# Attention over windows of 64 rows: VectorE and ScalarE as loops of three units with token semaphores, spare loads copied by GpSimd, stores issued later in the unit

## The chip, the cores and the metric

The kernel runs on one core of a Trainium2 chip. Sixteen DMA engines move data between HBM (the large memory) and the buffers on the chip; a transfer is *issued* by an instruction, waits its turn in a queue (18.9 to 29.2 us from issue to landing for v, q, k and the store, medians on the page of the kernel before), and has *landed* when all its data is there. The metric is the device time of one execution in microseconds (us), the median of several. The span printed on a profile page is some 1.8 us shorter than the device time of the same execution.

Executions of one and the same kernel scatter by about 2 us each way, and now and then by more. The times below are always given with the kernel before timed on the same chip in the same rounds.

## The reference

```python
# q, k, v: float32 [4, 4096, 1536]; windows of W = 64 rows
q_w, k_w, v_w = (x.reshape(B, S // 64, 64, D) for x in (q, k, v))
logits = einsum('bnwd,bnud->bnwu', q_w, k_w) * D ** -0.5
attn   = softmax(logits, axis=-1)
out    = einsum('bnwu,bnud->bnwd', attn, v_w).reshape(B, S, D)
```

Three inputs of 100.66 MB are read and one output of the same size is written. There is little arithmetic for each byte.

## The kernel before

The 16384 rows are cut into N = 32 units of 512 rows. For each unit:

1. GpSimd (POOL) issues loads of q, k and v, 3.15 MB each in HBM, on one queue that casts to fp16 on the way. `q16`, `k16` and `v16` have one buffer each, so a load can be issued only after TensorE (PE) has finished with the unit before.
2. PE transposes q and k; VectorE (DVE) and ScalarE (ACT) copy the results in turns to `xq` and `xk`; PE forms the logits; ACT takes exp.
3. The last stage has four rows, n = 0 to 3. In each, PE multiplies with v into three 128x512 outputs, with one more matmul for the sum of the exps. DVE takes the reciprocal of the sum, and DVE and ACT scale the outputs into one of three `outs` buffers.
4. POOL issues the store of the unit, 3.15 MB.

The first loads have special places, because nothing has come free yet: q and k of unit 1 go to `outs[2]`, v of unit 1 to `outs[1]`, v of unit 2 to `vs`. DVE copies them to `q16`, `k16` and `v16`. The parts that matter (cuts are marked `# ...`):

```python
def vector_unit(u):                        # unrolled, 32 times
    # ... six copies of transposes, waits on counts: p_t >= 6*u + ...
    src = {1: staged(1, 0), 2: vs, N - 1: vs}.get(u)
    if src is not None:                    # spare load of v
        # ... waits
        ve.tensor_copy(out=v16[:, :, :], in_=src[:, :, :]).then_inc(g_v, 1)
    if u == 0:                             # spare load of q
        ve.wait_ge(d_q1, 16)
        ve.wait_ge(p_t[1], 3)
        ve.tensor_copy(out=q16[:, :, :], in_=staged(2, 0)).then_inc(g_q, 1)
    for n in range(H * R):                 # the four rows of the last stage
        ve.wait_ge(p_s, 4 * u + n + 1)     # the sum is there
        ve.reciprocal(...).then_inc(n_r, 1)    # both DVE and ACT wait for n_r
        # ... scale DVE's share of the three outputs, each after its own p_o
    if u == 0:
        # ... the same for the spare load of k

# PE, last stage: the sum matmul follows the first output of each row
for j in range(NJ):
    # ... matmul of output j
    if j == 0:
        # ... sum matmul, tells p_s

# POOL
for u in range(1, N):
    gp.wait_ge(p_t[1], 6 * u + 3);  load("q", u + 1, q16, d_q)
    gp.wait_ge(p_t[1], 6 * u + 6);  load("k", u + 1, k16, d_k)
    store(u - 1)                           # waits for the scaling of unit u-1
    gp.wait_ge(p_o[0], 6 * u + 6); gp.wait_ge(p_o[1], 6 * u + 6)
    load("v", u + 1, v16, d_v)             # 2 < u + 1 < N - 1
```

The whole kernel:

The softmax here doesn't subtract the row's maximum and nothing guards it: scores larger than these inputs give would overflow.

Of the kernel before, what the change touches and what calls it, by code (L numbers as in the profile page):

```python
# [17 lines left out]
def kernel(  # L18
# [13 lines left out]
    PE = mybir.EngineType.PE  # L32
# [31 lines left out]
    zeros = sb("zeros", [P, 1], FP32)  # L64
# [12 lines left out]
    g_q, g_k, g_v, g_w = (sem(n) for n in ("g_q", "g_k", "g_v", "g_w"))  # L77
# [6 lines left out]
    n_r = sem("n_r")  # L84
# [45 lines left out]
    def tensor_unit():  # L130
        def transpose(g):
            src = q16 if g < DC else k16
            c = g % DC
            for i in range(SLOTS):
                r, j = i // H, i % H
                pairs = src[:, R * j + r, :].bitcast(FP32)
                if g == DC and i == 0:
                    nc.tensor.sem_inc(g_k, -1)._wait_ge(g_k, 1)
                ins = nc.tensor.transpose(  # L139
                    tps[g % 2][:, r, j, :], pairs[:, c * P : (c + 1) * P], ident[:, :]  # L140
                )
                if i == 0 and g >= 2:
                    ins._wait_ge(f_c[(g - 2) % 4], 1).then_inc(f_c[(g - 2) % 4], -1)
                if g == 0 and i == 0:
                    ins._wait_ge(g_q, 1)
                if g == 0 and i == 1:
                    ins.then_inc(g_q, -1)
                if i == SLOTS - 1:
                    ins.then_inc(p_t[g % 2], 1)

        def product(c):
            for h in range(H):
                for w in range(2):
                    for r in range(R):
                        ins = nc.tensor.matmul(  # L155
                            lts[h][:, r, :, :],
                            lhsT=halves(xk, c)[:, r, h, :, w],
                            rhs=halves(xq, c)[:, :, h, :, w],
                            start=(c == 0 and w == 0 and r == 0),
                            stop=(c == DC - 1 and w == 1),  # L160
                            skip_group_check=True,
                        )
                        if h == w == r == 0 and c >= DC - 2:
                            s = f_c[(DC + c) % 4]
                            ins._wait_ge(s, 1).then_inc(s, -1)
                        if c == DC - 1 and w == r == 1:
                            ins.then_inc(p_l, 1)

        for g in range(2 * DC):
            transpose(g)  # L170
            if g >= DC + 2:
                product(g - DC - 2)
        product(DC - 2)
        product(DC - 1)
        for n in range(H * R):
            h, t = n // R, n % R
            if n == 0:
                nc.tensor.sem_inc(g_v, -1)._wait_ge(g_v, 1)  # L178
            for r in range(R):
                w = ets[h][:, r, t, :]  # L180
                ld = nc.tensor.ldweights(w)  # L181
                if r == 0 and t == 0:
                    ld._wait_ge(f_x[h], 1)
                for j in range(NJ):
                    ins = reuse(
                        ops[j][:, :], w, v16[:, R * h + r, 512 * j : 512 * (j + 1)], r == 0, r == R - 1
                    )
                    if r == 0:
                        if n == 0 and j == 0:
                            ins._wait_ge(g_w, 1).then_inc(g_w, -1)  # L190
                        elif n > 0:
                            ins._wait_ge(f_o[j][n % 2], 1).then_inc(f_o[j][n % 2], -1)
                    if r == R - 1:
                        ins.then_inc(p_o[on_act(n, j)], 1)
                    if j == 0:
                        ins = reuse(sp[:, n : n + 1], w, ones[:, 0:1], r == 0, r == R - 1)
                        if r == 0 and t == 0:
                            ins.then_inc(f_x[h], -1)
                        if r == R - 1:
                            ins.then_inc(p_s, 1)  # L200

    def copy_out(eng, copy, u, g):
        xt = xq if g < DC else xk
        eng.wait_ge(p_t[g % 2], 6 * u + g // 2 + 1)
# [7 lines left out]
    def freed(eng, u):  # L212
        if u >= NO:
            eng.wait_ge(d_o[u % NO], 16 * (u // NO))

    def told(ins, n, j, a):
        if n == H * R - 1:
# [4 lines left out]
    def vector_unit(u):  # L222
        ve = nc.vector
        for g in range(0, 2 * DC, 2):
            copy_out(ve, ve.tensor_copy, u, g)
        src = {1: staged(1, 0), 2: vs, N - 1: vs}.get(u)
        if src is not None:
            ve.wait_ge(*((d_v1, 16) if u == 1 else (d_vs, 16 if u == 2 else 32)))
            ve.wait_ge(p_o[0], 6 * u)
            ve.wait_ge(p_o[1], 6 * u)  # L230
            ve.tensor_copy(out=v16[:, :, :], in_=src[:, :, :]).then_inc(g_v, 1)
        if u == 0:
            ve.wait_ge(d_q1, 16)
            ve.wait_ge(p_t[1], 3)
            ve.tensor_copy(out=q16[:, :, :], in_=staged(2, 0)).then_inc(g_q, 1)
        i = 0
        for n in range(H * R):
            ve.wait_ge(p_s, 4 * u + n + 1)
            ve.reciprocal(out=rs[:, n : n + 1], in_=sp[:, n : n + 1]).then_inc(n_r, 1)  # L239
            for j in range(NJ):  # L240
                if not on_act(n, j):
                    if i == 0:
                        freed(ve, u)
                    ve.wait_ge(n_r, 4 * u + n + 1)
                    ve.wait_ge(p_o[0], 6 * u + i + 1)
                    i += 1
                    told(
                        ve.tensor_scalar_mul(scaled(u, n, j), ops[j][:, :], scalar1=rs[:, n : n + 1]),  # L248
                        n, j, 0,
                    )  # L250
        if u == 0:
            ve.wait_ge(d_k1, 16)
            ve.wait_ge(p_t[1], 6)
            ve.tensor_copy(out=k16[:, :, :], in_=staged(2, 1)).then_inc(g_k, 1)

    def scalar_unit(u):
        sc = nc.scalar
        for g in range(1, 2 * DC, 2):
            copy_out(sc, sc.copy, u, g)
        for h in range(H):  # L260
            sc.wait_ge(p_l, 2 * u + h + 1)
            for a in range(0, P, W // R):
                s = slice(a, a + W // R)
                ins = sc.activation(  # L264
                    ets[h][s, :, :, s], lts[h][s, :, :, s], EXP, bias=zeros[s, :], scale=scale
                )
            ins.then_inc(f_x[h], 1)
        i = 0
        for n in range(H * R):
            for j in range(NJ):  # L270
                if on_act(n, j):
                    if i == 0:
                        freed(sc, u)
                    sc.wait_ge(n_r, 4 * u + n + 1)
                    sc.wait_ge(p_o[1], 6 * u + i + 1)  # L275
                    i += 1
                    told(
                        sc.activation(  # L278
                            scaled(u, n, j), ops[j][:, :], COPY, bias=0.0, scale=rs[:, n : n + 1]
                        ),  # L280
                        n, j, 1,
                    )

    def store(u):
        gp = nc.gpsimd
        gp.wait_ge(n_e[0], 2 * u + 2)
        gp.wait_ge(n_e[1], u + 1)
        gp.dma_start(  # L288
            out=rows(of, u * UR, SLOTS, R), in_=slots(outs[u % NO], 0, SLOTS, R)
        ).then_inc(d_o[u % NO], 16)  # L290

    with tc.tile_critical(no_gpsimd_drain=True):
# [26 lines left out]
        nc.scalar.activation(rs[:, 0:1], zeros[:, :], EXP, bias=zeros[:, :], scale=1.0)  # L319
# [8 lines left out]
        for u in range(N):  # L328
            vector_unit(u)
            scalar_unit(u)  # L330

        sy = nc.sync
        sy.sem_inc(g_w, 1)
# [3 lines left out]
        sy.wait_ge(d_k, 16)  # L337
        sy.sem_inc(g_k, 1)
        sy.wait_ge(d_v, 16)
        sy.sem_inc(g_v, 1)  # L340
        for u in range(1, N + 1):
            if 1 < u < N:
                sy.wait_ge(d_q, 16 * (u - 1))
                sy.sem_inc(g_q, 1)
                sy.wait_ge(d_k, 16 * u)
                sy.sem_inc(g_k, 1)
            if u < N:
                sy.wait_ge(n_e[0], 2 * u)
                sy.wait_ge(n_e[1], u)
                sy.sem_inc(g_w, 1)  # L350
            if 2 < u < N - 1:
                sy.wait_ge(d_v, 16 * (u - 1))
                sy.sem_inc(g_v, 1)

        gp = nc.gpsimd
        for u in range(1, N):
            if u + 1 < N:
                gp.wait_ge(p_t[1], 6 * u + 3)
                load("q", u + 1, q16, d_q)
                gp.wait_ge(p_t[1], 6 * u + 6)  # L360
                load("k", u + 1, k16, d_k)
            if u + 1 == N - 1:
                load("v", u + 1, vs, d_vs)
            store(u - 1)
            if 2 < u + 1 < N - 1:
                gp.wait_ge(p_o[0], 6 * u + 6)
                gp.wait_ge(p_o[1], 6 * u + 6)
                load("v", u + 1, v16, d_v)


        u, base, o = N - 1, (N - 1) * UR, outs[(N - 1) % NO]
        gp.wait_ge(p_o[1], 6 * u + 5)
        gp.wait_ge(p_o[0], 6 * u + 4)
        gp.dma_start(out=rows(of, base, R, R), in_=slots(o, 0, R, R)).then_inc(d_l[0], 16)
        gp.wait_ge(p_o[1], 6 * u + 6)
        gp.wait_ge(p_o[0], 6 * u + 6)
# [3 lines left out]
        for j, (a, c) in enumerate(((0, 2 * N - 1), (1, N), (0, 2 * N))):  # L380
# [43 lines left out]
```

## Time and profile before

| | before |
|---|---|
| device time, median of 3 | 948.83 us (948.52 to 949.06) |
| span of the profiled execution | 948.6 us |
| HBM traffic | 301.99 MB read, 100.66 MB written |
| mean rate over the span | 424 GB/s |
| PE / ACT / DVE / POOL busy | 67 / 36 / 32 / 9% |

The first lines of the page, the row of DMA digits (each the mean busy share of the DMA engines in one fortieth of the span, in tenths), and the line of HBM traffic, before:

```profile
span 948.6 us, 10199 instructions
...
PE 631.6 (67%) x4096; PEld 349.9 (37%) x3328; DVE 301.4 (32%) x524; ACT 341.2 (36%) x644; POOL 81.8 (9%) x133
...
DMA  9999999999999999999999999999999999999997
...
HBM read 301.99 MB, written 100.66 MB: 424 GB/s over the span
```

The row of nines is the main reading: the sixteen DMA engines are busy from the first slice to the last, and the busiest other engine, PE, is at 67%. From the packet records I read a steady rate of about 431 GB/s in the middle of the run, with reads counted at their size in HBM. A load writes only half of what it reads (fp16 for fp32), and it still takes as long as a store: 7.24 to 7.32 us of the queue for a load, 7.34 us for a store (medians, kernel before). So the time goes by the size in HBM here, and no run here shows which part of the path is the limit; that the transfers alone set the time is shown below (e4). The gap between 424 over the span and 431 is start, drain and a few short deficits.

Two groups of instructions, before: line, engine, operation, count, then busy time, mean ns, the idle time just before them and what ended most of it.

```profile
L114 PE MATMUL o<-v,et 128*128 128x512 f16 x768 | 257.5, 455 | 209.1 <-PEq L178 151.7
...
L107 POOL DMA_DIRECT2D v<-in_v_dram x29 | 20.8, 716 | 458.2 <-PE o L114 458.2
```

PE stands still for 151.7 us in front of the last stage, waiting for v (the wait on line 178, 28 times, 5.4 us each). This is the wait of the engine behind the DMA: a faster PE, DVE or ACT would mostly wait longer (with none of their work, e4 below, the whole time falls by 2.7 us).

So a change can help in three ways only: it can fill a hole in the DMA stream, shorten the start, or shorten the end. A hole arises when a load or store is issued so late that the queue has run dry. The issues of POOL's queue near the start, before (start, duration, line, what it moves, and the idle time of POOL with its releaser):

```profile
52.00 0.54 POOL L107 DMA_DIRECT2D q<-in_q_dram  x1 [39.94 <-PE tp L139]
58.73 0.87 POOL L107 DMA_DIRECT2D k<-in_k_dram  x1 [6.20 <-PE tp L139]
59.60 0.71 POOL L288 DMA_DIRECT2D out_dram<-out  x1
75.63 0.56 POOL L107 DMA_DIRECT2D q<-in_q_dram  x1 [15.31 <-PE tp L139]
82.23 0.87 POOL L107 DMA_DIRECT2D k<-in_k_dram  x1 [6.04 <-PE tp L139]
```

The q load at 75.63 us is that of unit 3, and it came when the queue was almost empty: a deficit of 1.9 us follows. It was the one hole I counted in the run apart from start and end.

The reciprocals of three rows in the middle of the run show the pace of the last stage, about 2.4 us a row before:

```profile
434.36 0.17 DVE L239 RECIPROCAL rs<-sp 128x1 f32<-128x1 f32 x1 [10.56 <-PE sp L114]
...
436.88 0.17 DVE L239 RECIPROCAL rs<-sp 128x1 f32<-128x1 f32 x1 [1.26 <-PE sp L114]
...
439.27 0.17 DVE L239 RECIPROCAL rs<-sp 128x1 f32<-128x1 f32 x1 [0.77 <-PE sp L114]
```

### The profile page before, as it was taken

The numbers are of one execution on the slowest core, as the hardware profiler recorded it, in microseconds if no ns is written. First come the engines' busy times: TensorE is split into PE (matmuls) and PEld (weight loads), VectorE is DVE, ScalarE is ACT, GpSimd is POOL, SyncE is SP. The second block draws the span as 40 slices with busy tenths as digits, with TensorE's granted clock in tenths as the row PEclk, the third lists the DMA queues.
The fourth block names the chain that finished last, engine by engine and source line by source line (L and its number), as shares of the span: only waits on it lengthen the run. The fifth ranks groups of instructions, "written<-read, shape, count | busy, mean of one in ns | idle before, by whom it ended". The sixth has DMA issues, their size and how long they took to land. (4 is left out here: it accounts for less than half of the span.)

```text
span 948.6 us, 10199 instructions
## 1 busy us (share of the span) xinstructions
PE 631.6 (67%) x4096; PEld 349.9 (37%) x3328; DVE 301.4 (32%) x524; ACT 341.2 (36%) x644; POOL 81.8 (9%) x133
## 2 busy tenths in 40 slices
PE   3687767766667576686666766667666677566683
PEld 2354444323443234442334432344323443234440
DVE  2434323322233322333222332223322233322342
ACT  2344434233333333333333433333333333333332
POOL 1000011010110000110001100011000110001100
PEclk9989999888899888988889998889988899888987
DMA  9999999999999999999999999999999999999997
GB/s 247 216 224 265 273 281 280 281 243 258 281 280 280 255 245 282 282 279 270 235 277 282 280 280 237 263 281 279 280 252 248 282 280 280 266 240 275 282 264 299
DMA packets 27234, 253.40 MB, mean 267 GB/s; under 512 B 2128, under 2 KB 2128, under 8 KB 10832
## 3 DMA queue, kind: packets, MB, share of 16 engines
q0 software_dynamic: 26496, 249.31, 100.2%
q1 hardware_dynamic: 720, 3.93, 1.1%
q14 instruction: 16, 0.13, 0.0%
q8 instruction: 2, 0.03, 0.0%
HBM read 301.99 MB, written 100.66 MB: 424 GB/s over the span
## 5 line engine op out<-in xcount | busy, mean ns | idle before, releaser
L114 PE MATMUL o<-v,et 128*128 128x512 f16 x768 | 257.5, 455 | 209.1 <-PEq L178 151.7
L278 ACT ACTIVATE out<-o,rs 128x512 f32<-128x512 f32 x192 | 126.9, 686 | 276.1 <-DVE rs L239 194.3
L155 PE MATMUL lt<-xq,xk 128*128 128x256 f16 x1536 | 196.3, 276 | 0.0
L181 PEld LDWEIGHTS <-et 128*128 128x128 f16 x256 | 29.3, 114 | 417.0 <-issue 411.4
L155 PEld LDWEIGHTS lt<-xq,xk 128*128 128x128 f16 x1536 | 149.2, 97 | 23.7
L239 DVE RECIPROCAL rs<-sp 128x1 f32<-128x1 f32 x128 | 21.6, 169 | 420.3 <-PE sp L114 420.3
L139 PE MATMUL tp<-ident,q 128*128 128x128 f32 x768 | 105.0, 281 | 61.7 <-DVE xq L206 49.0
L248 DVE TENSOR_SCALAR out<-o,rs 128x512 f32<-128x512 f32 x192 | 138.6, 748 | 16.4 <-PE o L114 10.0
L139 PE MATMUL tp<-ident,k 128*128 128x128 f32 x768 | 114.3, 279 | 33.1 <-DVE xk L206 13.2
L139 PEld LDWEIGHTS tp<-ident,q 128*128 128x128 f32 x768 | 87.3, 144 | 95.2 <-issue 80.3
L206 ACT COPY xk<-tp 128x512 f32<-128x512 f32 x96 | 59.0, 614 | 161.2 <-PE tp L139 161.2
L264 ACT ACTIVATE et<-lt,zeros 32x128 f16<-32x128 f32 x256 | 91.7, 358 | 56.1 <-PE lt L155 52.9
L206 DVE COPY xk<-tp 128x512 f32<-128x512 f32 x96 | 66.4, 692 | 125.5 <-PE tp L139 125.5
L139 PEld LDWEIGHTS tp<-ident,k 128*128 128x128 f32 x768 | 88.1, 142 | 48.7 <-issue 46.9
L206 ACT COPY xq<-tp 128x512 f32<-128x512 f32 x96 | 59.1, 615 | 93.5 <-PE tp L139 93.5
L206 DVE COPY xq<-tp 128x512 f32<-128x512 f32 x96 | 66.1, 689 | 55.0 <-PE tp L139 55.0
L107 POOL DMA_DIRECT2D v<-in_v_dram x29 | 20.8, 716 | 458.2 <-PE o L114 458.2
L114 PE MATMUL sp<-ones,et 128*128 128x1 f16 x256 | 46.3, 181 | 0.0
L107 POOL DMA_DIRECT2D k<-in_k_dram x31 | 17.7, 571 | 193.1 <-PE tp L139 186.1
L107 POOL DMA_DIRECT2D q<-in_q_dram x30 | 16.3, 542 | 163.1 <-PE tp L139 163.1
L288 POOL DMA_DIRECT2D out_dram<-out x31 | 22.1, 713 | 18.8 <-DVE out L248 17.8
L324 ACT CAST q<-out 128x1536 f16<-128x1536 f32 x2 | 2.9, 1472 | 6.9 <-DMA out<-in_q_dram 6.9
(22 smaller groups left out, 18.6 us busy)
## 6 DMA issues: line engine op xcount, KB each, us to landing
out_dram<-out POOLq DMA_DIRECT2D x31, 3072.0 KB, 29.2
k<-in_k_dram POOLq DMA_DIRECT2D x31, 1536.0 KB, 22.3
q<-in_q_dram POOLq DMA_DIRECT2D x30, 1536.0 KB, 21.6
v<-in_v_dram POOLq DMA_DIRECT2D x29, 1536.0 KB, 18.9
out<-in_q_dram SPq DMA_DIRECT2D x2, 1536.0 KB, 7.8
vs<-in_v_dram POOLq DMA_DIRECT2D x2, 1536.0 KB, 37.3
out<-in_q_dram POOLq DMA_DIRECT2D x1, 1536.0 KB, 25.1
out<-in_k_dram POOLq DMA_DIRECT2D x1, 1536.0 KB, 31.8
```

Source lines behind the costliest of these rows:

```text
L107: nc.gpsimd.dma_start(out=slots(dst, 0, SLOTS, r), in_=rows(src, u * UR, SLOTS, r)).then_inc(s, 16)
L114: return nc.tensor.add_instruction(mybir.InstMatmult(name=nc.get_next_instruction_name(), engine=PE, ins=[low(rhs), low(w)], outs=[low(o)] ...
L139: ins = nc.tensor.transpose(tps[g % 2][:, r, j, :], pairs[:, c * P : (c + 1) * P], ident[:, :])
L155: ins = nc.tensor.matmul(lts[h][:, r, :, :], lhsT=halves(xk, c)[:, r, h, :, w], rhs=halves(xq, c)[:, :, h, :, w], start=(c == 0 and w == 0 ...
L181: ld = nc.tensor.ldweights(w)
L206: copy(out=dst, in_=tps[g % 2][:, :, :, :]).then_inc(f_c[g % 4], 1)
L239: ve.reciprocal(out=rs[:, n : n + 1], in_=sp[:, n : n + 1]).then_inc(n_r, 1)
L248: ve.tensor_scalar_mul(scaled(u, n, j), ops[j][:, :], scalar1=rs[:, n : n + 1]),
L264: ins = sc.activation(ets[h][s, :, :, s], lts[h][s, :, :, s], EXP, bias=zeros[s, :], scale=scale)
L278: sc.activation(scaled(u, n, j), ops[j][:, :], COPY, bias=0.0, scale=rs[:, n : n + 1]),
L288: gp.dma_start(out=rows(of, u * UR, SLOTS, R), in_=slots(outs[u % NO], 0, SLOTS, R)).then_inc(d_o[u % NO], 16)
L324: copy(out=q16[:, i, :], in_=outs[0][:, i, :]).then_inc(c_q[a], 1)
```

## The change

It has four parts.

- **Loops.** DVE and ACT run ten iterations of three units, with the last two units written out, where they had 32 units unrolled. (PE was a loop already.) The waits in the loops are no longer on growing counts; each is a token: wait until the semaphore is at least 1, and take 1 away.
- **A longer hand-over.** The wait takes the token away, so a token has one taker. So the reciprocal signals DVE itself (`n_d`), DVE takes that token, and then gives ACT one (`n_r`). The sum matmul comes one output later (two in the last row), which lets some of the waits on outputs go.
- **GpSimd copies the first four spare loads**, so that DVE's loop has no special cases in it.
- **Stores later.** `store(u-1)` is issued when PE has begun the first row of unit u's last stage, rather than right after the k load. By then the scaling of unit u-1 is certainly done, and POOL needs no wait on DVE and ACT. The order of transfers on the queue stays the same. The two halves of the last store wait for PE's signals in the same way: the second half for the first output of row 3, and no longer for all of them.

The core of the diff, with cuts marked by `...`:

```diff
 # PE, last stage
+                at = NJ - 1 if n == H * R - 1 else 1
                 for j in range(NJ):
                     ...
-                    if j == 0:
+                    if j == at:
                         ins = reuse(sp[:, n : n + 1], w, ones[:, 0:1], r == 0, r == R - 1)
+    def await_(eng, s):
+        eng.sem_inc(s, -1)._wait_ge(s, 1)
 ...
 # DVE
         for n in range(H * R):
-            ve.wait_ge(p_s, 4 * u + n + 1)
-            ve.reciprocal(out=rs[:, n : n + 1], in_=sp[:, n : n + 1]).then_inc(n_r, 1)
+            await_(ve, p_s)
+            ve.reciprocal(out=rs[:, n : n + 1], in_=sp[:, n : n + 1]).then_inc(n_d, 1)
+            await_(ve, n_d)
+            ve.sem_inc(n_r, 1)
 ...
+        for eng, unit in ((DVE, vector_unit), (ACT, scalar_unit)):
+            with nc.Fori(0, N // NO, engines=OrderedEngineSet([eng]), head_slot={eng: 0}):
+                for u in range(NO):
+                    unit(u)
+            for u in range(N - 2, N):
+                unit(u)
 ...
 # POOL
+        gp.wait_ge(d_q1, 16)
+        gp.wait_ge(m_q, 1)
+        unstage(staged(2, 0), q16, g_q)       # gpsimd.tensor_copy
+        ... the same for k; v of units 1 and 2 inside the loop
-        for u in range(1, N):
-            ...
-            store(u - 1)
+        for u in range(1, N - 1):
+            ...
+            gp.wait_ge(m_k, u + 1)
+            load("k", u + 1, k16, d_k)
+            gp.wait_ge(m_0, u + 1)
+            store(u - 1)
+            ...
+                gp.wait_ge(m_v, u + 1)
+                load("v", u + 1, v16, d_v)
 ...
 # POOL, second half of the last store
-        gp.wait_ge(p_o[1], 6 * u + 6)
-        gp.wait_ge(p_o[0], 6 * u + 6)
+        gp.wait_ge(m_3, N)
```

`m_q`, `m_k`, `m_0`, `m_v` and `m_3` are signals that PE sends to POOL: after the last use of q, after the last use of k, at the first finished output of row 0, at the last use of v, the end of row 3, and at the first finished output of row 3.

## The prediction

The sum: it came to -1.7 + 1.3 + 0 to 0.4, that is -0.4 to 0 us.

> **What bounds it now.** The DMA. The page's HBM line: 301.99 MB read, 100.66 MB written, 424 GB/s over the span. The table of 10 us windows has a DMA share of 0.98 to 1.06 from 10 to 930 us. The engines are far from full (PE 67%, ACT 36%, DVE 32%, POOL 9%). POOL's timeline puts v-load issues at 120.13 and 882.51 us, 26 units apart: 29.3 us a unit for 12.58 MB, 429 GB/s. All large transfers go through one queue, in the order v, q, k, store, each issued about 12 us or more before its turn. PE waits for v: 151.7 us in 28 units, 5.4 us a unit (groups of instructions, idle column). So between 95 and 930 us a faster engine gains nothing.
>
> **What is left to gain.** From the packet records I count the deficit against the steady rate: about 1.9 us between 76 and 94 us (q for unit 3 issued at 75.63, when the queue was nearly empty), about 1.2 us between 932 and 936 us (before the first half of the last store is issued at 933.55), and start and drain (2 and 6 us), which the change leaves alone.
>
> **What the change does.**
> 1. GpSimd copies the four spare loads in place of DVE (1.75 us each). [...] DVE no longer waits for q1 (until 34.45 us, which held back unit 0's reciprocals by 4 us). I expect the next loads 4 to 6 us earlier (q2 near 47, q3 near 70), so the deficit at 76 to 94 us goes: -1.7 us.
> 2. Store later: issued about 435 in place of 425 us in the unit I read; its turn is at about 447. The order of transfers is the same and none starves: 0.
> 3. Loops for DVE and ACT: fewer instructions to fetch, but the page shows 0.13 MB on the instruction queue: 0. [...]
> 4. Tokens: the reciprocal takes one more semaphore hop to ACT (about 0.1 us), and the sum matmul comes one 128x512 matmul (0.21 us) later, two in the last row. Each of the four rows of the last stage grows by about 0.3 us, from 2.3 us. This is critical only from v of unit 30 (901.96 us) to the end: +1.3 us in unit 30, about +0.2 in unit 31 until the last store's first half is issued; at most 0.4 more after.
>
> Sum: -1.7 + 1.3 + 0 to 0.4: nearly nothing.
>
> **Predicted: 948.0 us, 8 in 10 between 945.8 and 950.2.** Faster by over 2%: 0.01; within 2%: 0.97; slower: 0.02.
>
> **What would show it.** (1) No windows below 400 GB/s (reads counted) between 76 and 94 us, and v of unit 30 landing 1 to 2 us earlier; (2) DMA share still 1.0, PE's wait for v still 4 to 5 us a unit; (3) last-stage rows of 2.6 us[...].
>
> **What would make it wrong.** GpSimd copies of over 8 us, which would hold the loads behind them in POOL's order; [...] a store issued so late that the queue runs dry; or rows that don't grow, which would leave a gain of 2 to 3 us.

## The result and the profile after

| | before | after |
|---|---|---|
| device time, median of 4 | 948.94 us (948.52 to 950.61) | 947.75 us (946.57 to 948.54) |
| ratio | | 0.9983 (95%: 0.9966 to 1.0) |
| span of the profiled execution | 948.6 us | 944.8 us |
| mean rate over the span | 424 GB/s | 426 GB/s |
| instructions | 10199 | 11112 |

A ratio is the mean time of one kernel's runs over that of the other's in the same rounds, so it is not quite the ratio of the medians. The change was timed twice more (e1 and e9 below): 0.9996 and 0.9991. All three intervals reach 1; taken together (mean 0.9990) they lean to a gain of about 0.1%, at the edge of what can be told from none. The predicted 948.0 us lies 0.25 us from the median.

The two spans differ by 3.8 us, and that must not be read as the effect of the change. The profiled execution of the kernel before took 950.37 us, at the upper end of its runs, and that of the kernel after took 946.57 us, the lowest of its runs.

The same lines of the page, after:

```profile
span 944.8 us, 11112 instructions
...
PE 628.2 (66%) x4128; PEld 352.7 (37%) x3360; DVE 294.3 (31%) x521; ACT 337.0 (36%) x645; POOL 92.1 (10%) x137
...
DMA  9999999999999999999999999999999999999998
...
HBM read 301.99 MB, written 100.66 MB: 426 GB/s over the span
```

Nothing has moved: the same bytes, and the same row of nines. The groups, after (line 117 is line 114 of before, line 110 was 107, line 284 is the store):

```profile
L117 PE MATMUL o<-v,et 128*128 128x512 f16 x768 | 244.8, 440 | 190.5 <-PEq L213 70.6
...
L110 POOL DMA_DIRECT2D v<-in_v_dram x29 | 20.8, 716 | 256.9 <-PE o L117 256.9
...
L284 POOL DMA_DIRECT2D out_dram<-out x31 | 22.1, 712 | 189.7 <-PE o L117 179.5
```

PE's wait for v has halved, from 151.7 us to 70.6 us (22 waits), and the time has not fallen. The slack that PE used to spend waiting for v is now partly spent within the unit, because each unit's chain is longer. POOL's wait before v (458.2, now 256.9 us) is split over the v load and the store, which now has a wait of its own of 179.5 us in 30 (6.0 us each).

The reciprocals of three rows, after:

```profile
433.48 0.17 DVE L241 RECIPROCAL rs<-sp 128x1 f32<-128x1 f32 x1 [6.98 <-DVEq L213]
...
436.26 0.17 DVE L241 RECIPROCAL rs<-sp 128x1 f32<-128x1 f32 x1 [1.51 <-DVEq L213]
...
439.16 0.17 DVE L241 RECIPROCAL rs<-sp 128x1 f32<-128x1 f32 x1 [1.08 <-DVEq L213]
```

A row takes 2.78 and 2.90 us where it took 2.52 and 2.39. This is where PE's slack went.

The start, after:

```profile
35.02 2.74 POOL L290 COPY q<-out 128x3072 f32<-128x3072 f32 x1 [22.89 <-DMA out<-in_q_dram]
42.28 2.75 POOL L290 COPY k<-out 128x3072 f32<-128x3072 f32 x1 [4.53 <-DMA out<-in_k_dram]
48.70 0.54 POOL L110 DMA_DIRECT2D q<-in_q_dram  x1 [3.67 <-PE lt L151]
49.59 2.75 POOL L290 COPY v<-out 128x3072 f32<-128x3072 f32 x1 [0.35 <-DMA out<-in_v_dram]
55.61 0.54 POOL L110 DMA_DIRECT2D k<-in_k_dram  x1 [3.27 <-PE lt L160]
60.53 0.71 POOL L284 DMA_DIRECT2D out_dram<-out  x1 [4.38 <-PE o L117]
69.28 2.75 POOL L290 COPY v<-vs 128x3072 f32<-128x3072 f32 x1 [8.04 <-PE o L117]
74.91 0.56 POOL L110 DMA_DIRECT2D q<-in_q_dram  x1 [2.88 <-PE lt L151]
```

The copies take 2.75 us each, 0.90 ns for each of the 3072 fp32 words of a partition; DVE took 1.75 us in the kernel before. The q load of unit 2 is issued 3.3 us earlier than before (48.70 against 52.00). But that of unit 3, the one in front of the hole, is issued only 0.7 us earlier (74.91 against 75.63). I had said 70.

The deficit against 431 GB/s between 66 and 94 us, worked out from the packet records, was 1.9 us before and is 2.0 us after. The hole has stayed.

POOL's last three issues, before and then after: the store of unit 30, and the two halves of the last store.

```profile
913.46 0.70 POOL L288 DMA_DIRECT2D out_dram<-out  x1 [17.84 <-DVE out L248]
933.55 0.57 POOL L374 DMA_DIRECT2D out_dram<-out  x1 [19.38 <-PE o L114]
936.01 0.54 POOL L378 DMA_DIRECT2D out_dram<-out  x1 [1.89 <-PE o L114]
```

```profile
911.21 0.70 POOL L284 DMA_DIRECT2D out_dram<-out  x1 [10.22 <-DVE zeros L255]
932.16 0.57 POOL L394 DMA_DIRECT2D out_dram<-out  x1 [20.25 <-PE o L117]
934.98 0.54 POOL L397 DMA_DIRECT2D out_dram<-out  x1 [2.24 <-PE o L117]
```

In the trace of before, v of unit 30 (the last to come by the normal way) landed at 901.7 us, and unit 31's last stage began 25.0 us after unit 30's. In that of after it landed at 898.6 us, and the two stages are 26.2 us apart. This looks like the predicted growth of the tail (+1.3 us), but the comparison is not fair: in the first trace the granted clock was 0.63 and 0.89 in parts of that stretch, and 1.00 all through in the second. Near the start, where both clocks were 1.00, the distance from a unit's first reciprocal to that of the next is 23.5 us before (63.45 to 86.94) and 26.2 us after (60.60 to 86.80). So the change (tokens, and the later sum matmul) lengthens a unit's chain by 2.7 us, twice what I had said.

### The profile page after: what moved, and what is told of

Same layout as the page of the kernel before. It is cut to its first block, busy times and chain, and to the rows that moved or that the text cites. A ratio compares the mean times of both kernels' runs of the same rounds, so it can differ in the third digit from the quotient of the medians.

```text
span 944.8 us, 11112 instructions
## 1 busy us (share of the span) xinstructions
PE 628.2 (66%) x4128; PEld 352.7 (37%) x3360; DVE 294.3 (31%) x521; ACT 337.0 (36%) x645; POOL 92.1 (10%) x137
## 5 line engine op out<-in xcount | busy, mean ns | idle before, releaser
L117 PE MATMUL o<-v,et 128*128 128x512 f16 x768 | 244.8, 440 | 190.5 <-PEq L213 70.6
L276 ACT ACTIVATE out<-o,rs 128x512 f32<-128x512 f32 x192 | 124.9, 684 | 267.8 <-ACTq L213 267.8
L188 PEld LDWEIGHTS <-et 128*128 128x128 f16 x256 | 25.4, 99 | 390.7 <-issue 367.5
L142 PE MATMUL tp<-ident,q 128*128 128x128 f32 x768 | 112.4, 294 | 83.8 <-DVE xq L219 71.1
L160 PEld LDWEIGHTS lt<-xq,xk 128*128 128x128 f16 x1536 | 149.3, 97 | 23.8
L142 PEld LDWEIGHTS tp<-ident,q 128*128 128x128 f32 x768 | 91.0, 151 | 120.7 <-issue 120.6
L110 POOL DMA_DIRECT2D v<-in_v_dram x29 | 20.8, 716 | 256.9 <-PE o L117 256.9
L284 POOL DMA_DIRECT2D out_dram<-out x31 | 22.1, 712 | 189.7 <-PE o L117 179.5
L151 PE MATMUL lt<-ones,et 128*128 128x1 f16 x32 | 5.5, 171 | 0.0
## 6 DMA issues: line engine op xcount, KB each, us to landing
out<-in_q_dram POOLq DMA_DIRECT2D x1, 1536.0 KB, 25.6
```

Of the source, the lines that this page charges most:

```text
L110: nc.gpsimd.dma_start(out=slots(dst, 0, SLOTS, r), in_=rows(src, u * UR, SLOTS, r)).then_inc(s, 16)
L117: return nc.tensor.add_instruction(mybir.InstMatmult(name=nc.get_next_instruction_name(), engine=PE, ins=[low(rhs), low(w)], outs=[low(o)] ...
L142: ins = nc.tensor.transpose(tps[g % 2][:, r, j, :], pairs[:, c * P : (c + 1) * P], ident[:, :])
L151: nc.tensor.matmul(lts[0][:, 0, 0, 0:1], lhsT=ets[0][:, 0, 0, :], rhs=ones[:, 0:1], start=True, stop=True, skip_group_check=True,).then_in ...
L160: ins = nc.tensor.matmul(lts[h][:, r, :, :], lhsT=halves(xk, c)[:, r, h, :, w], rhs=halves(xq, c)[:, :, h, :, w], start=(c == 0 and w == 0 ...
L188: ld = nc.tensor.ldweights(w)
```

## Two measures that the experiments use

The trace records when each of the 16 DMA engines has finished its part of a transfer. They do not finish together: from first to last of the 16, the landings of one load are 1.7 us apart at 20 us and 5.6 us apart at 900 us in the kernel before, and 3.6 us at v of unit 30 in the kernel after. So a statement such as "the queue has 12 us of work left" is a different number for each engine.

**Margin**: the time from the issue of a transfer to the moment at which the *fastest* engine finishes the transfer ahead of it. Medians in the steady part (130 to 880 us), worked out from issue times and landings:

| margin, us | q | k | v | store |
|---|---|---|---|---|
| before | 11.4 | 12.1 | 8.7 | 18.8 |
| after | 9.0 | 9.1 | 7.2 | 9.4 |

The change spends 9.4 us of the store's margin, and 1.5 to 3 us of each load's. None of it reaches zero. For unit 3's q, the one behind the hole, the margin is 1.5 us before and 2.2 us after.

**Lag**: the landing of a transfer, less 7.29 us (the steady step of the queue) times its number in the queue. It stays constant while an engine is busy without a gap at its usual pace, and rises by whatever is lost. The lag of the slowest engine decides the end of the run; that of the fastest shows the holes. It will be given at k of unit 3 (just behind the hole) and at the last load, for the slowest and the fastest engine.

## The experiments

My theory after the result: the transfers alone set the time; the longer hand-over costs nothing in the middle, but eats the gain of GpSimd's copies in the first units, and costs about 1 us in the tail. (The part on the tail fell, as the table of lags below shows.) The rivals: the loops cost or save something (fetch of instructions), and the store's later issue costs something by itself. Three calls of four kernels each follow; the kernels of one call share a chip and the runs of the kernel before.

### Is there anything to gain, and do the loops matter? (first call)

**e1_after_again**: the changed kernel, not edited.

> The changed kernel, unedited, to learn its scatter. All theories: 946.5 to 948.5 us, ratio to the kernel before 0.997 to 1.000. Drift theory (each 8 KB instruction fetch holds one of the 16 DMA engines for about 0.31 us, the engines drift apart, and the end waits for the slowest): 16 engines' landings of v for unit 30 spread over 3 to 4.5 us (3.6 in the first trace, 5.6 in the kernel before), last landing about 3 us earlier than in the kernel before's trace.

Measured: 948.39 us (946.73 to 952.38) against 948.81 us (945.98 to 950.37), ratio 0.9996 (0.9979 to 1.0013). Its profiled execution was its slowest, 952.38 us. In that one the TensorE clock was at half speed just in unit 30's last stage, here in windows of 8 us (the number before the last two is the granted clock):

```profile
904.00:912.00 8.00, 6.07 (x19) 0.53 (x5) 2.67 (x6) 1.95 (x3) 0.72 (x1) 0.50 1.02 216
912.00:920.00 8.00, 5.69 (x25) 2.62 (x17) 3.63 (x7) 2.94 (x6) 0.70 (x1) 0.64 1.03 242
```

```profile
904.31 0.17 DVE L241 RECIPROCAL rs<-sp 128x1 f32<-128x1 f32 x1 [7.97 <-DVEq L213]
908.03 0.17 DVE L241 RECIPROCAL rs<-sp 128x1 f32<-128x1 f32 x1 [2.44 <-DVEq L213]
911.77 0.17 DVE L241 RECIPROCAL rs<-sp 128x1 f32<-128x1 f32 x1 [1.93 <-DVEq L213]
915.94 0.17 DVE L241 RECIPROCAL rs<-sp 128x1 f32<-128x1 f32 x1 [3.00 <-DVEq L213]
```

Rows of 3.7 to 4.2 us, rather than 2.8 to 3.0, delay the last store's first half to 939.04 us (932.16 in the first trace). In this trace even the slowest engine had only 0.6 us of work left at that moment, so this delay is in the time. It is one cause of scatter among others, and a reason why one profile of each kernel says nothing at this level.

**e2_unrolled**: the changed kernel, with the loops of DVE and ACT unrolled again.

```diff
         for eng, unit in ((DVE, vector_unit), (ACT, scalar_unit)):
-            with nc.Fori(0, N // NO, engines=OrderedEngineSet([eng]), head_slot={eng: 0}):
-                for u in range(NO):
-                    unit(u)
-            for u in range(N - 2, N):
+            for u in range(N):
                 unit(u)
```

> The changed kernel with the VectorE and ScalarE loops written out, tokens, GpSimd copies and store order kept: about 2300 more instructions[...]. Drift theory: the spread of v of unit 30 goes from about 3.6 to 5 or 6 us and the time rises by 1.0 to 2.5 us over the changed kernel of the same rounds. My prediction's view (loops are worth 0, gain came from the start and the tail): within 0.5 us of the changed kernel, spread unchanged.

Measured: 948.64 us (945.84 to 950.1), ratio 1.0003 (0.9985 to 1.002). The instruction queue moved 20 packets, 0.16 MB, against 8 packets, 0.07 MB in the looped kernel. So the loops do save fetches, and the fetches cost nothing that shows in this scatter (the changed kernel of the same call took 948.39 us). I had also suspected them of driving the DMA engines apart, since each is a single packet of 8 KB (0.31 to 0.32 us in the packet records of before and after from 20 us on, which is the figure of the drift theory): that idea fell here. The spread at v of unit 30 is 4.5 us with 20 fetches, and it was 5.6 us in e1 with 8.

At the loop's back edge in the trace of the kernel after, DVE's next copy follows its last scaling exactly as it does inside the body (416.65 us after a scaling at 415.33, and at the back edge 443.94 after 442.62: 1.32 us in both). No stall shows with bodies of three units (110 recorded instructions on DVE). PE's slack (2.5 us a unit in this trace) would have hidden a small one anyway.

**e3_padded**: the changed kernel, with 1920 extra instructions on SyncE that do nothing but add and take away a semaphore's value.

```diff
                 if n:
                     sy.sem_inc(g, 1)._wait_ge(d, 16 * n)
+            for _ in range(32 if 0 < u < N - 1 else 0):
+                sy.sem_inc(pad, 1)
+                sy.sem_inc(pad, -1)
```

> The changed kernel with 64 empty semaphore additions per unit on SyncE, which idles there: 1920 more instructions, about 15 more fetches of 8 KB, no other work. Drift theory: spread of v of unit 30 at 5 to 8 us, time up by 1.5 to 4 us over the changed kernel. Rival (loops helped, if at all, through the compute engines' own fetch or branch timing, not through the DMA): no change within 0.5 us.

Measured: 957.2 us (952.55 to 963.56), ratio 1.0081 (1.0054 to 1.0109). This is 8.8 us slower than e1, with only 23 packets on the instruction queue, 15 more than e1 and three more than e2. So it is not the number of fetches. In its trace v's margin is down to 5.3 us (median; the lowest is 0.8), and the slowest engine's lag grows by 14 us over the run, in many steps of 0.3 to 1 us. Why idle semaphore traffic does this is open; the experiment added more than the thing it was to vary, and says nothing about the change.

**e4_dma_floor**: the transfers of the changed kernel in their order, with nothing else. (The last three pieces, on SyncE, are issued some 18 us earlier than in the changed kernel.) It gives a wrong result: PE, DVE and ACT do no work apart from clearing the buffers that are stored, and each load waits for the load before it into the same buffer.

```diff
-            tensor_unit()                  # and all of DVE's and ACT's units
         ...
-            gp.wait_ge(m_q, u + 1)
+            if u > 1:
+                gp.wait_ge(d_q, 16 * (u - 1))
             load("q", u + 1, q16, d_q)
```

> All the loads and stores of the kernel through the same queues in the same order, no compute (result wrong on purpose): the time of the transfers alone. Drift theory: the slowest engine is busy from about 14 us to the end in the changed kernel too, so taking all compute away gains 1 to 4 us (943.5 to 946.5), part of it from the shallow queue between 66 and 92 us. Rival (compute chains at the start and in the last unit set the end): gains 4 to 8 us, 940 to 943.5.

Measured: 946.08 us (945.52 to 946.62), ratio 0.9975 (0.9959 to 0.999).

```profile
span 943.9 us, 198 instructions
...
DMA  9999999999999999999999999999999999999997
...
HBM read 301.99 MB, written 100.66 MB: 427 GB/s over the span
```

Bare transfers take 2.7 us less than the kernel before (948.81 minus 946.08). By this run, a change that leaves the transfers alone can be worth about 0.3% (0.1 to 0.4% by the interval). The bare transfers also scatter by half a microsecond each way, not by two.

### Which part does what? (second call)

**e5_gp_alone**: the kernel before with only GpSimd's copies: no tokens, no loops, stores as before.

```diff
-        if u == 0:
-            ve.wait_ge(d_q1, 16)
-            ve.wait_ge(p_t[1], 3)
-            ve.tensor_copy(out=q16[:, :, :], in_=staged(2, 0)).then_inc(g_q, 1)
         ... the copies of k and of v in units 1 and 2 go likewise
         gp = nc.gpsimd
+        gp.wait_ge(d_q1, 16)
+        gp.wait_ge(p_t[1], 3)
+        unstage(staged(2, 0), q16, g_q)
+        ... k, and inside the loop v of units 1 and 2, likewise
```

> The kernel before, with only its four spare copies moved from VectorE to GpSimd: no tokens, no loops, stores where they were. Margin theory (the transfers bind; what counts outside the steady state is how long the queue still runs when the next load is issued, 1.5 us at unit 3's q in the kernel before and 2.2 us in the changed one): copies of 2.75 us, unit 3's q issued near 70 us with 5 us or more of queue left, few slow packets between 66 and 92 us, time 0.5 to 2 us below the kernel before (946.5 to 948.5). Rival (the start is not worth anything): same as before within 0.5 us.

Measured: 947.61 us (946.97 to 949.34) against 949.03 us (947.79 to 953.45), ratio 0.9986 (0.9969 to 1.0003). POOL's issues of q for units 2 and 3:

```profile
46.65 0.54 POOL L107 DMA_DIRECT2D q<-in_q_dram  x1 [1.29 <-PE tp L139]
...
70.15 0.56 POOL L107 DMA_DIRECT2D q<-in_q_dram  x1 [1.96 <-PE tp L139]
```

These are what the prediction had said of the whole change (near 47, near 70). The margin of unit 3's q is 6.7 us here, against 1.5 before and 2.2 after. The distance from unit 1's first reciprocal to this issue is 12.2 us here (57.98 to 70.15), 12.2 us in the kernel before (63.45 to 75.63) and 14.3 us after (60.60 to 74.91). So the copies do what I expected of them, and the longer chains of units 0 and 1 undo it by unit 3. (No run takes out the tokens alone; e6 and e10 below put back only the place of the sum matmul.)

**e6_rows_short**: the changed kernel, with the sum matmul back at j = 0 (except in the last row), and the waits on outputs that this needs.

```diff
-                at = NJ - 1 if n == H * R - 1 else 1
+                at = NJ - 1 if n == H * R - 1 else 0
 ...
-                    if j == NJ - 1 and n != H * R - 1:
+                    if j > 0 and n != H * R - 1:
                         await_(ve, p_o[0])
 ...
-                    if j == NJ - 1:
+                    if j > 0 and n != H * R - 1:
                         await_(sc, p_o[1])
```

> The changed kernel with the sum matmul moved back behind the first 128x512 matmul of a row (three of four rows), and the tokens this needs. Rows of the last stage fall from 2.8 or 2.9 us to about 2.55. Margin theory: unit chain 0.6 to 1 us shorter, unit 3's q with 1 to 2 us more queue left, last unit 0.5 to 1 us earlier, time 0 to 1.5 us lower than the changed kernel's 948.4 in the last call. Rival (all of this is hidden): no change within 0.5 us.

Measured: 946.88 us (945.85 to 947.95), ratio 0.9976 (0.996 to 0.9993). This is as far below 948.4 us as the expectation allowed, though that figure is from another chip.

**e7_rows_long**: the changed kernel, with two idle reciprocals before each real one, to lengthen the hand-over further.

```diff
             await_(ve, p_s)
+            for i in range(2):
+                ve.reciprocal(out=idle[:, i : i + 1], in_=ones32[:, i : i + 1])
             ve.reciprocal(out=rs[:, n : n + 1], in_=sp[:, n : n + 1]).then_inc(n_d, 1)
```

> The changed kernel with two idle one-column reciprocals ahead of each row's own: each row about 0.4 us longer, a unit's chain about 1.6 us longer. Hidden in the steady state (queue runs on for 7 us at v's issue, would be 5.5), but exposed in the first three units and in the last two: time up by 1.5 to 5 us. If everything is hidden: no change within 0.5 us.

Measured: 949.99 us (947.1 to 956.61), ratio 0.9996 (0.9978 to 1.0015). The median lies 2.4 and 3.1 us above those of e5 and e6 of the same call, but the ratio can't be told from 1. The idle pair takes 0.22 us, and the rows near the start (2.91, 3.01 and 3.17 us) are only 0.11 to 0.13 us longer than in the changed kernel, not 0.4; the distance from unit 1's first reciprocal to unit 2's is 26.7 us, from 26.2. Its trace, of its slowest run (956.61 us), shows the mechanism in the open. The q load of unit 3 is issued only at 77.67 us, 0.9 us after the fastest engine had nothing left, and the DMA share (next to last number) falls in the windows after it:

```profile
76.00:80.00 4.00, 2.63 (x22) 2.29 (x23) 1.51 (x3) 1.72 (x3) 0.56 (x1) 1.00 0.68 175
80.00:84.00 4.00, 4.00 (x39) 3.61 (x37) 1.38 (x2) 0.62 (x1) 0.00 (x0) 1.00 0.91 194
84.00:88.00 4.00, 2.88 (x26) 2.23 (x23) 0.00 (x0) 2.02 (x5) 0.53 (x1) 1.00 1.12 197
```

**e8_store_latest**: the changed kernel, with the store issued still later, at the end of PE's last stage and not at its first row. The v load follows it at once, since it waits for the same signal.

```diff
-            gp.wait_ge(m_0, u + 1)
+            gp.wait_ge(m_v, u + 1)
             store(u - 1)
```

> The changed kernel with each store issued another 9 us later, at the end of the last stage, just ahead of v's load; order of the transfers unchanged. In the changed kernel the queue runs on for 9.4 us (fastest engine) and 12.8 us (slowest) when a store is issued; here it would be about 0.4 and 3.7 us, less than the 1 us or so from issue to first packet on the fast engines. Margin theory: fast engines run dry each unit, slow packets after each store's issue, time up by 2 to 10 us. Rival (only the order counts, the margin is never used up): no change within 0.5 us.

Measured: 991.67 us (990.91 to 993.38), ratio 1.0446 (1.0425 to 1.0466): 43 us slower than the kernel before. The wait of POOL before the store, in the view of waits (total, times, longest), and the windows around one such store, issued at 434.50 us:

```profile
POOL out_dram L284 <- PE o L117: 519.2, 30, 19.7
```

```profile
430.00:435.00 5.00, 4.05 (x21) 1.06 (x10) 1.29 (x4) 1.44 (x3) 0.50 (x1) 0.80 0.94 199
435.00:440.00 5.00, 2.64 (x18) 2.31 (x17) 2.95 (x5) 1.63 (x3) 0.92 (x2) 0.88 0.86 354
```

The wait is 17.3 us a store (519.2 by 30), where it was 6.0 in the kernel after. The store's margin has a median of 0.8 us and a lowest of -0.8 us. The DMA share dips at each unit, about 1.4 us are lost a unit (43 us by 30), and the lag, which grows by 46 us over the run for the slowest and the fastest engine alike, is the whole loss. The engines' spread shrinks to 0.45 us at v of unit 30: when the queue runs dry, the fast engines wait and the others catch up.

### Repeats, and the edge of the store's cliff (third call)

**e9_after_third**: the changed kernel, not edited.

> The changed kernel once more, beside the next three on one chip. From the two sets so far (ratios to the kernel before 0.9983 and 0.9996): ratio 0.997 to 1.001. If the change is worth nothing of its own: interval holds 1. If it gains 0.1 to 0.2 per cent: 0.998 to 0.999 with an interval below 1.

Measured: 949.09 us (945.93 to 950.16) against 949.82 us (947.72 to 951.51), ratio 0.9991 (0.9975 to 1.0006).

**e10_rows_short_again**: e6 again.

> The changed kernel with shorter rows, as before (ratio 0.9976 then). Margin theory: again 0.997 to 0.9985, 0.5 to 1.5 us under the changed kernel of this call. If the last result was the chip's scatter: equal to the changed kernel within 0.3 us, ratio above 0.999.

Measured: 946.74 us (945.77 to 947.62), ratio 0.9965 (0.9953 to 0.9978). The means of this call are 948.55 us for the changed kernel and 946.65 us for this one: 1.9 us less on the same chip. It is the only version that is faster than the kernel before in both of its calls with an interval below 1. Its rows near the start, from the reciprocals:

```profile
61.27 0.17 DVE L241 RECIPROCAL rs<-sp 128x1 f32<-128x1 f32 x1 [5.72 <-DVEq L213]
...
63.84 0.17 DVE L241 RECIPROCAL rs<-sp 128x1 f32<-128x1 f32 x1 [1.18 <-DVEq L213]
...
66.54 0.17 DVE L241 RECIPROCAL rs<-sp 128x1 f32<-128x1 f32 x1 [0.89 <-DVEq L213]
```

Rows of 2.57 and 2.70 us, against 2.78 and 2.90 in the changed kernel at this place (60.60, 63.38, 66.28) and 2.32 and 2.39 before (63.45, 65.77, 68.16): about two fifths of what was added is back in these two rows. A whole unit takes 25.6 us (61.27 to 86.88), from 26.2.

**e11_gp_alone_again**: e5 again.

> The kernel before with GpSimd's copies alone, as before (ratio 0.9986 then). If the start's copies are what the change gains by, and its longer rows give some of it back: ratio 0.998 to 0.999 again, at or a little below the changed kernel. If scatter: ratio above 0.9995.

Measured: 947.82 us (946.37 to 949.64), ratio 0.9984 (0.9971 to 0.9997). The q load of unit 3 is issued at 68.7 us with a margin of 8.2 us.

**e12_store_mid**: the store issued between those of the changed kernel and of e8, at the third row of the last stage.

```diff
-            gp.wait_ge(m_0, u + 1)
+            gp.wait_ge(m_2, u + 1)
             store(u - 1)
```

> The changed kernel with each store issued two rows later (about 5.6 us), order unchanged. The queue should run on for about 3.6 us (fastest engine) and 7 us (slowest) at the store's issue, still more than the time from issue to first packet. Margin theory: no change beyond 1 us, where the 9 us delay cost 43 us. If the cost goes with the delay: about 25 us more.

Measured: 965.9 us (960.34 to 969.81), ratio 1.0167 (1.0135 to 1.0198), 16 us slower than the kernel before (965.9 minus 949.82) and 17 us slower than the changed one. My expectation missed. I had taken the median of the margin that this issue would leave, and the median was indeed harmless (3.6 us). But units in which the TensorE clock is low have a longer last stage (rows of 3.7 to 4.2 us at 0.50 to 0.64 in e1, 2.78 to 3.05 us at 1.00 in the trace of the kernel after), so that the store is issued later. From 130 us on, every store with a margin of 0.7 to 2 us follows 9 us in which the granted clock was 0.50 to 0.60. 18 transfers with a margin under 4 us carry 16.0 of the 18.9 us that its stream lost in all (by the median of the engines).

### What a late issue costs, and who pays

First, all transfers from k of unit 2 on, issued before 895 us, of all profiled executions except e4's: how much later than one step of 7.29 us each landed after the one ahead (median of its engines), by the margin at its issue. In brackets the number of transfers.

| margin, us | q: extra us | k | v | store |
|---|---|---|---|---|
| under 0 | 2.4 (1) | | | 2.9 (7) |
| 0 to 1 | 1.5 (3) | | 1.7 (1) | 2.0 (12) |
| 1 to 2 | 0.2 (3) | | 1.0 (4) | 1.0 (10) |
| 2 to 3 | 0.4 (2) | 1.3 (8) | 0.2 (4) | 0.4 (10) |
| 3 to 4 | 0.0 (4) | 0.6 (5) | -0.2 (11) | 0.4 (4) |
| 4 to 5 | 0.0 (20) | 0.4 (15) | -0.1 (32) | 0.4 (8) |
| 7 to 8 | 0.0 (48) | 0.1 (48) | -0.1 (99) | 0.1 (46) |

Below 1 us of margin a transfer loses 1.5 to 3 us; between 1 and 2 us a store or a v load still loses about 1 us; above some 4 us it is at most 0.4. (q loads with 1 to 2 us lose only 0.2 themselves, but the k load right behind, with 2 to 3 us, loses 1.3, and carries part of their loss.) A part of this is the time from the issue to the first packet. It can be read where engines had run dry: 1.2 to 1.3 us, the "1 us or so" of the expectation for e8 (before, first half of the last store, issued at 933.55 us; e7, q of unit 3, at 77.67; e8, the store at 434.50). Most of the short margins are in e3, e8 and e12, and this is a correlation over transfers; but e8 and e12 moved the issue on purpose, and fit it.

Second, the lag, for the profiled execution of each kernel. The next column is the landing of the last piece of the last store, less the slowest engine's lag at the last load: what the tail adds. The last column is the same with the end of the program in place of that landing.

| | k of unit 3: slowest, fastest | last load: slowest, fastest | tail | to the end |
|---|---|---|---|---|
| before | 22.8, 20.4 | 26.9, 21.3 | 919.1 | 921.7 |
| after | 22.9, 19.9 | 23.8, 20.2 | 919.2 | 921.0 |
| e1, changed kernel again | 22.5, 21.1 | 27.8, 22.2 | 920.7 | 922.8 |
| e9, and again | 22.6, 20.0 | 24.4, 20.4 | 919.2 | 921.0 |
| e2, unrolled | 21.5, 18.8 | 23.5, 19.0 | 918.8 | 920.6 |
| e5, copies alone | 21.4, 18.8 | 23.3, 19.0 | 919.4 | 922.0 |
| e11, copies alone again | 21.4, 18.5 | 22.9, 18.8 | 919.2 | 921.7 |
| e6, rows short | 22.0, 18.7 | 23.6, 18.9 | 918.8 | 920.5 |
| e10, rows short again | 22.9, 20.2 | 24.8, 20.8 | 918.8 | 920.8 |
| e7, rows long | 23.5, 22.4 | 31.6, 26.9 | 921.9 | 923.3 |

Four things are to be read there.

- **The hole at unit 3**: its lag is the same before and in the changed kernel (22.8; 22.9, 22.5, 22.6), and about 1.4 us less with the copies alone (21.4 twice). It is not there in every execution with tokens: in e2, whose chains are the long ones too, unit 1's stage happened to begin earlier (first reciprocal at 58.96 us; 59.94, 60.60 and 61.30 in the changed kernel; e6 and e10, one kernel, are 2.1 us apart there), q3 was issued at 73.48 us with 4.0 us of margin, and the lag is 21.5. The longer chains put q3 at the edge of the hole, and the start's own scatter decides.
- **The tail, to the last landing**: it is the same to 0.1 us before and after (919.1; 919.2, 919.2), although the last store's first half is released by a chain that is 2.7 us longer. The slowest engine hides it: at that issue it still has 5.0 us of the store of unit 30 to do in the trace of before, and 3.4 us in that of after. Only the fast engines wait. In e1, where the clock fell in the tail, it had 0.6 us left, in e7 it had been out of work for 0.6 us, and there the tail costs 1.5 and 2.7 us more than in the others.
- **The very end**: in all these traces the program ends 3.4 us after POOL's half of the last store has landed, and not a fixed time after the last landing, which is that of a piece on SyncE. In the changed kernel POOL issues this half 0.3 us before the last reciprocal (934.98 against 935.28), where it did so 1.0 us after it (936.01 against 935.04). The half then lands 1.7 us before the last piece, where it was 0.8 us. So to the end of the program the tail is 0.7 us *shorter*: 921.7 to 922.0 in the three traces with the old wait (before, e5, e11), 920.5 to 921.0 in five of those with the new one. In the other two, e1 and e7, the chain that releases the last store came later still (see above). That the earlier issue is the reason is argued from these traces; no run changes it alone.
- **The scatter**: between these two places the slowest engine loses 0.9, 5.3 and 1.7 us in three executions of one and the same kernel (23.8-22.9, 27.8-22.5, 24.4-22.6, with rounding), while the fastest loses 0.3 to 1.1. This drift of single engines is larger than all effects of the change, and makes most of the 3.8 us between the first two traces (4.0 us before, 0.9 after); the very end makes 0.7 of the rest.

## Why the prediction was right

The time was right (948.0 predicted; 947.75 measured, inside the range), and so were the class and the main reason for it: the DMA bounds the kernel, and what the change does to the engines happens under it. Bare transfers take 946.08 us (e4). But the sum that led to 948.0 has two terms that were both off, by about as much, in opposite directions; that the number came out so near is in part luck. Point by point:

1. **GpSimd's copies: right by themselves, mis-sized in the change.** The copies took 2.75 us. The prediction said "I expect the next loads 4 to 6 us earlier (q2 near 47, q3 near 70), so the deficit at 76 to 94 us goes: -1.7 us." With the copies alone this is what happens (46.65 and 70.15 us, 1.4 us less lag, ratios 0.9986 and 0.9984). In the whole change q2 came 3.3 us earlier, q3 only 0.7 us, and the lag at unit 3 is that of before. **This term measured about 0 in place of -1.7 us.** The step that failed: I counted the longer hand-over in the tail alone. It acts in the first units too, where the queue is short: from the first reciprocal of unit 1 to q3's issue take 12.2 us without tokens and 14.3 us with them.
2. **The store: right, for a reason that was too generous.** I compared its issue with its turn, 12 us away, and called it free. The fastest engine reached its end 9.4 us after the issue, and the slowest 12.8. It was still free. But the edge is near: 5.8 us less margin costs 17 us over the run (e12), 8.6 us less costs 43 (e8).
3. **Loops: right, within the scatter.** Nothing that shows, by e2 (948.64 us unrolled, 948.39 us looped).
4. **Tokens: right mechanism, both sizes wrong.** The matmul's part, put at 0.21 us, is 0.215 us from start to start at full clock in both traces. The hop's part was put at about 0.1 us; from a reciprocal's end to ACT's next scaling the trace of before has 0.10 us (median) and that of after 0.28 us, so it came to nearly 0.2. Rows were to grow by about 0.3 us; they grew by 0.5 to 0.8 us near the start (2.32, 2.39 and 2.24 us before, 2.78, 2.90 and 3.05 after). Transposes grew as well, which I had not costed: a pair takes 1.61 us, from 1.50. A unit's chain grew by 2.7 us and not by 1.3. But **the tail measured about -0.7 us in place of +1.3**: to the last landing it is the same to 0.1 us, since the slowest DMA engine is still busy when the longer chain ends, and the end of the program comes 0.7 us sooner, with the earlier issue of the last store's second half. For that stretch I had said at most 0.4 us more. I had called the tail critical because the *queue* looked empty; it was empty for the fast engines only.

So the sum by the traces is about 0 - 0.7, where mine was -1.7 + 1.3 to 1.7. Both are nearly nothing at this size. A gain of 0.7 us is a ratio of 0.9993; the three measured ones, 0.9983, 0.9996 and 0.9991, agree with it, and each alone can't be told from 1.

The sign that I had named, v of unit 30 landing 1 to 2 us earlier, was a bad one: in three traces of the changed kernel it landed at 898.6, 902.6 and 899.2 us. It varies with the drift of the engines by more than the effect. And PE's wait for v, said to stay at 4 to 5 us a unit, fell to 2.5 us (70.6 us over 28 units), again because the chain is longer.

The best version is the changed kernel with its rows made short again (e6, e10): 0.9976 and 0.9965, both below 1. Its 946.74 us is 0.7 us above the bare transfers (946.08, though on another chip). Much below that, only a change to the transfers themselves could go.

**What stays open.** Why single DMA engines fall back in a queue that never runs dry, and why by a different amount in each execution: the fetch of instructions is ruled out as the main cause (e2). Why 1920 idle semaphore instructions make it much worse (e3). And where the 1.9 us come from by which e10 beats the changed kernel of its call: the lag at unit 3 and the tail account for 1.1 us in the trace of e6 and for nothing in that of e10 (lags of 22.0 and 22.9 against a mean of 22.7; to the end 920.5 and 920.8 against 921.0), so one trace each does not divide it.

## What to carry to other kernels

Before tuning a kernel bound by its DMA, run its transfers alone: the distance to that time is all that any change on the engines can win, and here it was 0.3%. Judge a later issue by the time until the *fastest* DMA engine runs out of work, in the slowest units and not in the median one (here some 4 us were enough, and under 1 us cost 1.5 to 3 us each time), and judge the end of the run by the *slowest* engine, which may hide a longer tail (here a chain 2.7 us longer). Measure the tail to the end of the program, not to the last landing (here they differ by 0.7 us). A longer hand-over between engines was free here where the queue was deep (margins of 7.2 us and more in the steady part), and not at unit 3's q (14.3 us from unit 1's first reciprocal to its issue, in place of 12.2): count it in the first units too.
